# Down-projection of a decoder layer's FFN: 8 block products per pair, or 7 by a Strassen scheme between the next group's up tiles

## The chip, the core and the metric

The kernel runs on one core of one Trainium2 chip. The metric is the device time of one execution in microseconds; lower is better. Five engines work side by side, each through its own instructions in order: TensorE (PE, with its weight loads as PEld), VectorE (DVE), ScalarE (ACT), GpSimd (POOL) and SyncE (SP). SyncE does no arithmetic here, it issues DMAs; the 16 DMA engines of the core move the bytes.

## The reference: one layer with an FFN

One decoder layer over 256 tokens of 2048 channels: a mixing part (convolution, pooling, cross-attention), its output projection, and an FFN with 5632 hidden channels. All is float32. What the change touches is the FFN's last step:

```python
        h = rmsnorm(x, g_ffn[l])
        u = causal_dwconv(h @ w_up[l], ffn_conv_w[l]) + ffn_conv_b[l]
        gate, val = jnp.split(u, 2, axis=-1)
        x = x + (jax.nn.silu(gate) * val) @ w_down[l]
    return rmsnorm(x, g_final)
```

## The kernel before, and how its work is staged

Float32 products are made on TensorE from operands in two float32r parts, hi and lo, with hi x hi + hi x lo + lo x hi, three matmuls for one. Activations stay in SBUF with both parts side by side; weights are streamed. A weight tile of 1 MB (128 x 2048 floats) is loaded by SyncE into one of three `raw` buffers (`load`, L108), then `split_piece` (L121) has ScalarE copy it to `hi` (L129) and VectorE subtract to get `lo` (L130). `hi` and `lo` have three buffers each. `next_tile` (L149) hands tiles out in the order of a list, `stream`, and issues loads three tiles ahead and splits two tiles ahead of use.

The FFN runs over 22 units of 256 hidden channels. `up(u, gi)` makes a unit: four weight tiles, two for the gate and two for the value (`unit_a`, `mm_a`: pairs of a 512-column and a 256-column matmul, L306 and L309), and after each half `up_finish`: copy from PSUM and add (`gather`, L322 to L324), convolution over tokens (L747, L751), silu (L755). The product of gate and value is split and put into the group's tile `u` (L776 to L778). GpSimd sets the two margin columns of each half's rows (L743) in six rotating buffers.

Units form groups of 8, 7, 5 and 2 (`UNITS`, L157). A group's down-projection, `down` (L782), comes after the first unit of the next group, that of the third group after all units. For each half of the 2048 output columns it runs `mm_b` (L326) over tiles of two chunks of 128 hidden channels: 24 matmuls of 512 columns for a tile (L338, L341, L344), with four accumulators in PSUM (two token blocks by two column blocks of 512). At the end of the half `add_in` (L702) adds them to the residual `xt` (L706). The last group of two units goes through `down_last` (L793), with the final norm and the output stores. In between, the scheduler places instructions on each engine by priority; the first and last parts keep the order of the program.

```python
    UNITS = [8, 7, n_units - 17, 2]  # sizes of FFN groups in units of 256 channels
...
    def next_tile():
        i = state["use"]
        state["use"] += 1
        advance(i + 1 + LOAD_AHEAD, i + 1 + SPLIT_AHEAD)
        return split.pop(i)
```

Of the kernel before, what the change touches and what calls it, by code (L numbers as in the profile page):

```python
# [24 lines left out]
def kernel(  # L25
# [45 lines left out]
    # Per-channel vectors, as columns of 128 channels, by transposing rows of 128.  # L71
# [20 lines left out]
    rows = lambda v: v.rearrange("(r c) -> r c", c=P)  # noqa: E731  # L92
# [10 lines left out]
    stream = []  # (source, nk, ncol, pieces)  # L103
# [52 lines left out]
    n_units = NF // 2  # L156
    UNITS = [8, 7, n_units - 17, 2]  # sizes of FFN groups in units of 256 channels  # L157
# [20 lines left out]
    # The pool's weights: per pair of groups the three chunks' rows, in the columns of  # L178
    # the output chunks that they reach; wp_at[k] is the first of them.
# [17 lines left out]
    # Chunks of the mix in the order in which they come about.  # L197
# [10 lines left out]
    # A group's down-projection comes after the next group's first unit; that of the  # L208
    # last but one after all units.
    sched = []  # L210
    done = 0
    for gi, (a, n) in enumerate(group_of):
        upto = n_units if gi + 2 >= len(group_of) else a + n + 1
        for u in range(done, upto):
            sched.append(("up", u, [g for g, (b, m) in enumerate(group_of) if b <= u][-1]))
        done = upto
        sched.append(("down", gi, None))
    for what, a, b in sched:
        if what == "up" and a == 0:
            for h in (0, 1):  # L220
                plan_a(w_up, 0, (h,))
                plan_a(w_up, D_UP, (h,))
        elif what == "up":
            plan_a(w_up, a * 256)
            plan_a(w_up, D_UP + a * 256)
        else:
            a0, n = group_of[a]
            for n2 in range(2):
                plan_b(w_down, a0 * 2, n * 2, n2 * 1024, 1024, 2)

# [89 lines left out]
    def gather(ps, row, o, engine=nc.vector):  # L320
        """(main + corrections) * row -> o [P, S] in SBUF."""
        nc.scalar.activation(o, ps[:, S:], AF.Copy)  # L322
        nc.vector.tensor_tensor(o, ps[:, :S], o, op=ALU.add)
        engine.tensor_tensor(o, o, row, op=ALU.mult)  # L324
# [44 lines left out]
    # The order of the first instructions is that in which the data arrive.  # L369
# [66 lines left out]
    def split_into(o, src, n=S):  # L436
        """float32 [P, n] -> o, its two parts one after the other."""
# [50 lines left out]
    # 1 / (number of tokens averaged) for the first tokens  # L488
# [73 lines left out]
    # The sums run on GpSimd while the next unit's products do; the rest comes after.  # L562
    pending = []

    def pool_sums(ps, i):
# [3 lines left out]
        spans = []  # (first row, last row, group) of this chunk  # L569
# [17 lines left out]
    def pool_means():  # L587
        for i, v, spans, sums in pending:
# [11 lines left out]
            # The convolution's chunks of the mix are free until it comes.  # L600
# [122 lines left out]
    row_2 = None  # L723
    u_tiles = {}

    def up_matmul(u):
        if u:
            return [unit_a(h2T, f"g{u}"), unit_a(h2T, f"v{u}")]
        ps = [[bank(f"pu0_{w}_{mi}") for mi in range(2)] for w in range(2)]
        for h in range(2):  # L730
            for w in range(2):
                mm_a(ps[w], next_tile(), h2T, h * 8, 8, h == 0, h == 1)
                if h == 0 and w == 0:
                    transpose_in(xt, h2T, "g_ffn", range(8, 16), "x2")
        return ps

    def up_finish(ps, u, w):
        """main + corrections, norm, convolution and bias of one half of a unit."""
# [20 lines left out]
    def up(u, gi):  # L759
        nonlocal row_2  # L760
        if gi not in u_tiles:
            u_tiles[gi] = apool.tile([P, 16, 2 * S], F32R, tag="act", name=f"u_{gi}")
        ut = u_tiles[gi]
        base = group_of[gi][0]
        if u == 0:
            ps_g, ps_v = up_matmul(0)
            row_2 = row_of(rstd_sum(ssq4, "x2"), "x2")
            gates = up_finish(ps_g, u, 0)
        else:
            ps_g = unit_a(h2T, f"g{u}")  # L770
            gates = up_finish(ps_g, u, 0)
            ps_v = unit_a(h2T, f"v{u}")
        vals = up_finish(ps_v, u, 1)
        for mi in range(2):
            c = (u - base) * 2 + mi
            nc.vector.tensor_tensor(gates[mi], gates[mi], vals[mi], op=ALU.mult)  # L776
            nc.scalar.activation(ut[:, c, :S], gates[mi], AF.Copy)
            nc.vector.tensor_tensor(  # L778
                ut[:, c, S:], gates[mi], ut[:, c, :S].bitcast(F32), op=ALU.subtract
            )  # L780

    def down(gi):  # L782
        ut = u_tiles[gi]
        nk = group_of[gi][1] * 2
        for n2 in range(2):
            ps = [[bank(f"pd_{gi}_{n2}_{tb}_{n}") for n in range(2)] for tb in range(TB)]
            for i in range(nk // 2):
                mm_b(ps, next_tile(), ut, (2 * i, 2 * i + 1), range(TB), i == 0, i == nk // 2 - 1)
            add_in(ps, n2 * 2, range(TB), f"d{gi}")

    # The last group goes by token blocks and column pieces, each followed by its share
    # of the final norm, so that little is left after the last product.
    def down_last(gi):  # L793
        ut = u_tiles[gi]
# [3 lines left out]
        nc.scalar.activation(gfin, gfin, AF.Copy, scale=-0.5)  # goes with -2 / sqrt  # L798
# [28 lines left out]
        def partial(tb):  # L827
            """The mean square + eps, but for the last piece."""
# [4 lines left out]
        def rstd_last(tb):  # L833
            """-2 / sqrt(mean square + eps), with a Newton step."""
# [20 lines left out]
        with tc.manual_schedule(engines=IN_ORDER):  # L855
# [32 lines left out]
    for what, a, b in sched:  # L888
        if what == "up":
            up(a, b)  # L890
        elif a < len(group_of) - 1:
            down(a)
        else:
            down_last(a)
# [31 lines left out]
```

## Time and profile before

| | before |
|---|---|
| time, median of 3 runs | 1064.57 us (1064.54 to 1064.72) |
| profiled execution: span | 1064.7 us |
| instructions | 14249 |
| moved by DMA | 202.01 MB, 190 GB/s in the mean |
| VectorE, most waited for | lo on ACT's hi: 270.6 us in 168 waits |

The profile comes from one execution. Busy time is given for each engine; the span is cut into 40 slices whose digits are busy tenths; PEclk is the clock granted to TensorE in tenths of full speed. A group row reads: line, engine, operation, what is written and read, shape, count | busy us, mean ns of one | idle time of the engine just before, and what ended it. The chain that ended last follows the work back from the last instruction to whatever released it. No accumulating DMA and no DMA issued by GpSimd is in this profile.

### The profile page before, as it was taken

The page shows a single profiled execution, that of the slowest core. Times are in us where ns is not written, and L with a number is a line of the kernel's source. Part 1 is how long each engine was busy: PE and PEld are TensorE (multiplying, and loading weights), DVE is VectorE, ACT ScalarE, POOL GpSimd, SP SyncE. Part 2 cuts the span into 40 slices and gives each one's busy share as a digit, 9 for nine tenths or more (in the row PEclk, how much of TensorE's full clock was granted, in tenths as well). Part 3 has the DMA queues.
Part 4 walks back from the last instruction along what each step waited for, and adds up shares of the span by engine and source line. Part 5 has one row for each costly group of instructions (what it writes and reads, how often), then busy time and mean ns, then how long its engine had stood idle before and what let it go on. Part 6 is the DMA issues. An engine that isn't in the chain of part 4 may idle for free.

```text
span 1064.7 us, 14249 instructions
## 1 busy us (share of the span) xinstructions
PE 1054.7 (99%) x5632; PEld 907.2 (85%) x5632; DVE 703.6 (66%) x920; ACT 529.0 (50%) x683; POOL 43.1 (4%) x163
## 2 busy tenths in 40 slices
PE   9999999999999999999999999999999999999996
PEld 8888898888888888888888888888888888888885
DVE  5677786764556777777744467777754477777655
ACT  5965454443446655555533344554533345555343
POOL 0023500000000000000000000000000000000000
PEclk9999999999999999999999999999999999999998
DMA  9765465455555556555555555655555555654552
GB/s 316 243 224 172 143 206 189 161 195 183 186 185 174 184 196 198 188 181 185 198 198 198 196 171 187 198 185 175 195 198 197 191 174 190 198 177 178 198 198 80
DMA packets 147342, 202.01 MB, mean 190 GB/s; under 512 B 3619, under 2 KB 125771, under 8 KB 147147
## 3 DMA queue, kind: packets, MB, share of 16 engines
q1 hardware_dynamic: 147242, 201.09, 55.8%
q8 instruction: 44, 0.72, 0.3%
q14 instruction: 24, 0.19, 0.0%
q10 hardware_dynamic: 32, 0.01, 0.0%
HBM read 198.99 MB, written 2.10 MB: 189 GB/s over the span
## 4 chain that ended last, share of the span: by engine, by line
PE 98%; DVE 1%; ACT 0%; issue 0%; DVEq 0%
PE pa_v L306 15%; PE pa_g L306 15%; PE pa_g L309 7%; PE pa_v L309 7%; PE pd L338 7%; PE pd L344 7%; PE pd L341 7%; PE po L338 3%; PE po L341 3%; PE po L344 3%; PE pa_cc L306 2%; PE pa_cx L306 2%; PE pa_cb L306 2%; PE pa_pv L306 2%; PE pk L395 2%; PE pa_q L306 1%
## 5 line engine op out<-in xcount | busy, mean ns | idle before, releaser
L130 DVE TENSOR_TENSOR lo<-raw,hi 128x2048 fp32r<-128x2048 f32 (+2 forms) x196 | 425.5, 2172 | 271.6 <-ACT hi L129 270.6
L129 ACT ACTIVATE hi<-raw 128x2048 fp32r<-128x2048 f32 (+2 forms) x196 | 355.9, 1818 | 255.8 <-PE pd L344 98.4
L306 PE MATMUL pa_v<-h2T,hi 128*128 128x512 f32 x672 | 236.7, 396 | 0.0
L306 PE MATMUL pa_g<-h2T,hi 128*128 128x512 f32 x672 | 236.7, 396 | 0.0
L309 PE MATMUL pa_g<-h2T,lo 128*128 128x256 f32 x672 | 188.5, 281 | 0.0
L309 PE MATMUL pa_v<-h2T,lo 128*128 128x256 f32 x672 | 188.5, 281 | 0.0
L306 PEld LDWEIGHTS pa_v<-h2T,hi 128*128 128x128 f32 x672 | 126.0, 188 | 30.0
L306 PEld LDWEIGHTS pa_g<-h2T,hi 128*128 128x128 f32 x672 | 126.0, 188 | 30.0
L309 PEld LDWEIGHTS pa_g<-h2T,lo 128*128 128x128 f32 x672 | 127.0, 189 | 0.1
L309 PEld LDWEIGHTS pa_v<-h2T,lo 128*128 128x128 f32 x672 | 127.0, 189 | 0.0
L338 PE MATMUL pd<-hi,u 128*128 128x512 f32 x320 | 98.6, 389 | 0.0
L341 PE MATMUL pd<-lo,u 128*128 128x512 f32 x320 | 98.5, 389 | 0.0
L344 PE MATMUL pd<-hi,u 128*128 128x512 f32 x320 | 98.5, 389 | 0.0
L751 DVE SCALAR_TENSOR_TENSOR t<-h,cols,t 128x256 f32<-128x256 f32 x176 | 79.1, 480 | 2.2 <-ACT t L747 1.4
L755 ACT ACTIVATE t<-t 128x256 f32<-128x256 f32 x44 | 18.3, 418 | 107.0 <-DVE t L751 107.0
L341 PEld LDWEIGHTS pd<-lo,u 128*128 128x128 f32 x320 | 60.1, 188 | 12.6
L344 PEld LDWEIGHTS pd<-hi,u 128*128 128x128 f32 x320 | 60.1, 188 | 12.4
L338 PEld LDWEIGHTS pd<-hi,u 128*128 128x128 f32 x320 | 59.9, 188 | 12.4
L747 ACT ACTIVATE t<-h,cols 128x256 f32<-128x256 f32 x88 | 49.8, 593 | 0.0
L322 ACT ACTIVATE h<-pa_g 128x256 f32<-128x256 f32 x42 | 16.0, 380 | 61.3 <-PE pa_g L309 61.3
L338 PE MATMUL po<-hi,mixT 128*128 128x512 f32 x128 | 39.6, 391 | 0.0
L341 PE MATMUL po<-lo,mixT 128*128 128x512 f32 x128 | 39.5, 389 | 0.0
(207 smaller groups left out, 1280.9 us busy)
## 6 DMA issues: line engine op xcount, KB each, us to landing
raw<-in_w_up_dram SPq DMA_DIRECT2D x88, 1024.0 KB, 5.0
raw<-in_w_down_dram SPq DMA_DIRECT2D x44, 1024.0 KB, 4.9
raw<-in_w_in_dram SPq DMA_DIRECT2D x28, 1024.0 KB, 4.9
raw<-in_w_out_dram SPq DMA_DIRECT2D x16, 1024.0 KB, 4.9
raw<-in_w_kv_dram SPq DMA_DIRECT2D x4, 1024.0 KB, 5.2
raw<-in_w_kv_dram SPq DMA_DIRECT2D x6, 512.0 KB, 8.3
memt<-in_mem_dram SPq DMA_DIRECT2D x8, 256.0 KB, 7.7
xt<-in_x_dram SPq DMA_DIRECT2D x4, 512.0 KB, 6.7
```

The lines of the kernel that those rows point to most:

```text
L129: nc.scalar.activation(hi[:, s, :], raw[:, s, :], AF.Copy)
L130: nc.vector.tensor_tensor(lo[:, s, :], raw[:, s, :], hi[:, s, :].bitcast(F32), op=ALU.subtract)
L306: nc.tensor.matmul(ps[mi], hi[:, kk, c], actT[:, k, :], start=first and kk == 0, stop=False)
L309: nc.tensor.matmul(ps[mi][:, S:], lo[:, kk, c], actT[:, k, :S], start=False, stop=last and kk == nk - 1,)
L322: nc.scalar.activation(o, ps[:, S:], AF.Copy)
L338: nc.tensor.matmul(ps[tb][n], ah, hi[:, kk, c], start=f, stop=False)
L341: nc.tensor.matmul(ps[tb][n], ah, lo[:, kk, c], start=False, stop=False)
L344: nc.tensor.matmul(ps[tb][n], al, hi[:, kk, c], start=False, stop=l)
L395: nc.tensor.matmul(psk[mi], wt[0][:, j, c], mT[:, k, :], start=k == 0, stop=False)
L747: nc.scalar.activation(t, hp[:, 2:], AF.Identity, bias=cvec("ffn_conv_b", m), scale=cw[2])
L751: nc.vector.scalar_tensor_tensor(t, hp[:, s : s + S], cw[s], t, op0=ALU.mult, op1=ALU.add)
L755: nc.scalar.activation(t, t, AF.Silu)
```

## The change

The FFN's groups become five of 4 units and a last one of 2. For each of the five groups the down-projection is done in two halves of 1024 columns (`Blocks`, p = 0 and 1). In each, the activations are taken as 2 x 2 blocks (two token blocks of 128; even and odd chunks of hidden channels, four chunks each), and so are the weights (even and odd chunks; two column blocks of 512). Instead of 8 block products 7 are made, each of 4 chunks x 3 matmuls of 512 columns. The left operands are sums and differences of activation blocks, made by `turn` on VectorE and ScalarE once per group into the tile `sums`; the right ones are sums of weight blocks, made in place in three 1 MB buffers of the tile `ffn` by DMAs from SBUF to SBUF that add to their destination, issued by GpSimd:

| product | left | right | buffer steps after its split |
|---|---|---|---|
| 0 | a11 | b11 | b11 += b12; b12 += b22 |
| 1 | a21 - a22 | b11 + b12 | b11 += b22 |
| 2 | a21 - a22 - a11 | b11 + b12 + b22 | |
| 3 | a11 - a21 | b12 + b22 | load b21 over b12; b11 += b21 |
| 4 | a12 + a21 - a22 - a11 | b22 | load the next pair's b11 |
| 5 | a12 | b21 | load the next pair's b22 |
| 6 | a22 | b11 + b12 + b22 + b21 | load the next pair's b12 |

Each product's PSUM bank is added to or subtracted from a block of `xt` right away; some products go on in the bank of an earlier one. A group's 14 products stand between the next group's 16 up tiles: none after the first three, one after each of the next twelve, two after the last. In the last group, which has eight up tiles, it is one after each of six, two after the seventh and six after the eighth. The comments are left out too.

```diff
     def load(i, between=None):
         src, nk, ncol, pieces = stream[i]
+        if nk is None:
+            return
...
-    UNITS = [8, 7, n_units - 17, 2]  # sizes of FFN groups in units of 256 channels
+    UNITS = [4] * ((n_units - 2) // 4) + [2]
...
+        def buf(self, name):
+            at = {"b11": 0, "b22": 1, "b12": 2, "b21": 2}[name]
+            return rawd[(self.seq + at) % 3]
...
+        def add(self, to, what):
+            nc.gpsimd.dma_start(self.buf(to), self.buf(what), accum_op=ALU.add)
+
+        def split(self, i, idx):
+            raw = self.buf(("b11", "b11", "b11", "b12", "b22", "b21", "b11")[idx])
+            hi, lo = split[i] = [
+                wpool.tile([P, 4, 512], F32R, tag=t, name=f"{t}_{i}") for t in ("hi", "lo")
+            ]
+            nc.scalar.activation(hi, raw, AF.Copy)
+            nc.vector.tensor_tensor(lo, raw, hi.bitcast(F32), op=ALU.subtract)
+            if idx == 0:
+                self.add("b11", "b12")
+                self.add("b12", "b22")
+            elif idx == 1:
+                self.add("b11", "b22")
+            elif idx == 3:
+                self.load("b21")
+                self.add("b11", "b21")
+            elif self.next is not None and idx >= 4:
+                self.next.load({4: "b11", 5: "b22", 6: "b12"}[idx])
...
+        if not prods:
+            after = [0] * n_t
+        elif n == 4:
+            after = [0, 0, 0] + [1] * 12 + [2]
+        else:
+            after = [1, 1, 1, 1, 1, 1, 2, 6]
...
+        for at, src in parts:
+            nc.scalar.activation(sums[:, at, 0], src, AF.Copy)
+        tt(t[:, 0], a21, a22, op=ALU.subtract)
+        tt(t[:, 2], a11, a21, op=ALU.subtract)
+        tt(t[:, 1], t[:, 0], a11, op=ALU.subtract)
+        for at, src in parts[:1]:
+            tt(sums[:, at, 1], src, sums[:, at, 0].bitcast(F32), op=ALU.subtract)
+        tt(t[:, 3], t[:, 1], a12, op=ALU.add)
+        nc.scalar.activation(sums[:, 1:5, 0], t, AF.Copy)
+        for at, src in parts[1:]:
+            tt(sums[:, at, 1], src, sums[:, at, 0].bitcast(F32), op=ALU.subtract)
+        tt(sums[:, 1:5, 1], t, sums[:, 1:5, 0].bitcast(F32), op=ALU.subtract)
...
+    def prod(bl, i):
+        hi, lo = next_tile()
...
+        for j in range(4):
+            ah, al = sums[:, i, 0, j, :], sums[:, i, 1, j, :]
+            for n, (a, b) in enumerate(((ah, hi), (ah, lo), (al, hi))):
+                nc.tensor.matmul(
+                    ps, a, b[:, j, :], start=first and j == 0 and n == 0,
+                    stop=j == 3 and n == 2, skip_group_check=True,
+                )
+        c0 = bl.p * 1024 + right * 512
+        o = xt[:, tb, c0 : c0 + 512]
+        nc.vector.tensor_tensor(o, o, ps, op=op)
```

How the instructions then stand is decided by the scheduler. On ScalarE, in the middle of the FFN, this is the stretch of one unit before: `hi` is a weight split, `h` the copy from PSUM, `t` the convolution or silu. In brackets are the semaphores waited for; DMAHW are the loads.

```order
L322 ACTIVATE h_0_0_4157<-pa_g_0_4079 128x256 [waits PE_49,Pool_49]
L129 ACTIVATE hi_4181<-raw_4119 128x2048 [waits DMAHW3_49,PE_49,Activation_49]
L747 ACTIVATE t_0_0_4162<-h_0_0_4157,cols 128x256 [waits DVE_49]
L322 ACTIVATE h_0_1_4167<-pa_g_1_4080 128x256 [waits PE_49,Pool_49]
L755 ACTIVATE t_0_0_4162<-t_0_0_4162 128x256 [waits DVE_49]
L129 ACTIVATE hi_4219<-raw_4179 128x2048 [waits DMAHW4_49,PE_49,Activation_49]
```

The same engine after the change, at the first three products of a group's first pair. L131 splits an up tile, L247 a product's weight block out of the tile `ffn`; DMASW are the adding DMAs that GpSimd issued.

```order
L247 ACTIVATE hi_4837<-ffn 128x2048 [waits DMAHW1_49,Activation_49]
L131 ACTIVATE hi_4875<-raw_4835 128x2048 [waits DVE_49,DMAHW6_49,PE_49,Activation_49]
L808 ACTIVATE t_0_0_4818<-h_0_0_4813,cols 128x256 [waits DVE_49]
L808 ACTIVATE t_0_1_4828<-h_0_1_4823,cols 128x256 [waits DVE_49]
L816 ACTIVATE t_0_0_4818<-t_0_0_4818 128x256 [waits DVE_49]
L816 ACTIVATE t_0_1_4828<-t_0_1_4828 128x256 [waits DVE_49]
L387 ACTIVATE h_1_0_4911<-pu_1_0_4833 128x256 [waits PE_49,Pool_49]
L387 ACTIVATE h_1_1_4920<-pu_1_1_4834 128x256 [waits PE_49,Pool_49]
L808 ACTIVATE t_1_0_4916<-h_1_0_4911,cols 128x256 [waits DVE_49]
L808 ACTIVATE t_1_1_4925<-h_1_1_4920,cols 128x256 [waits DVE_49]
L247 ACTIVATE hi_4933<-ffn 128x2048 [waits DMASW0_49,Activation_49]
L131 ACTIVATE hi_4954<-raw_4931 128x2048 [waits DMAHW7_49,PE_49,Activation_49]
```

A product's split now stands ahead of each up tile's split, and that of product 1 (hi_4933) waits for an adding DMA, with the next up tile's split behind it.

On GpSimd there were only the margins of the up rows (L743) in this part. Now the adds (L240) stand among them (L804), here those of a first pair's products 0 and 1:

```order
L240 DMA ffn<-ffn 128x2048 [waits DMAHW5_49,DMAHW3_49,DMAHW7_49,DMAHW0_49,DVE_49]
L804 MEMSET h_1_0_4124 128x2 [waits DVE_49,Activation_49,Pool_49]
L804 MEMSET h_1_1_4133 128x2 [waits DVE_49,Activation_49,Pool_49]
L240 DMA ffn<-ffn 128x2048 [waits DMAHW1_49,DMASW0_49]
L804 MEMSET h_0_0_4259 128x2 [waits DVE_49,Activation_49,Pool_49]
L804 MEMSET h_0_1_4269 128x2 [waits DVE_49,Activation_49,Pool_49]
L240 DMA ffn<-ffn 128x2048 [waits DVE_49]
```

The second add (b12 += b22) waits until the first (b11 += b12) has landed, the third (b11 += b22) for VectorE's split of product 1.

At the end of the FFN, ScalarE's row of splits for the last pair, products 1 to 6, and the first tile of the last group's down-projection (L131); L387 and L808 belong to the last up tile, L503 splits the last units' result:

```order
L247 ACTIVATE hi_8370<-ffn 128x2048 [waits DMASW4_49,PE_49,Activation_49]
L387 ACTIVATE h_1_0_8425<-pu_1_0_8311 128x256 [waits PE_49,Pool_49]
L387 ACTIVATE h_1_1_8434<-pu_1_1_8312 128x256 [waits PE_49,Pool_49]
L808 ACTIVATE t_1_0_8430<-h_1_0_8425,cols 128x256 [waits DVE_49]
L808 ACTIVATE t_1_1_8439<-h_1_1_8434,cols 128x256 [waits DVE_49]
L503 ACTIVATE h2T<-t_0_0_8277 128x256 [waits DVE_49]
L247 ACTIVATE hi_8389<-ffn 128x2048 [waits DMASW6_49,Activation_49]
L503 ACTIVATE h2T<-t_0_1_8287 128x256 [waits DVE_49]
L247 ACTIVATE hi_8453<-ffn 128x2048 [waits DMASW5_49,Activation_49]
L247 ACTIVATE hi_8473<-ffn 128x2048 [waits DMAHW5_49,PE_49,Activation_49]
L247 ACTIVATE hi_8490<-ffn 128x2048 [waits DMAHW1_49,DVE_49,PE_49]
L247 ACTIVATE hi_8509<-ffn 128x2048 [waits DMASW7_49,DVE_49,PE_49]
```

Products 1, 2, 3 and 6 wait for adds (DMASW), and no up tile's split stands between them; the last group's tiles come behind.

More of the change, by code (lines that the diff above doesn't have):

```diff
@@ L156 @@
     n_units = NF // 2
[L157 removed]
+    UNITS = [4] * ((n_units - 2) // 4) + [2]
+    assert sum(UNITS) == n_units
     D_UP = DFF
@@ L210 @@
+    blocks = []
+    for gi in range(len(group_of) - 1):
+        for p in range(2):
+            blocks.append(Blocks(len(blocks), gi, p))
+            if len(blocks) > 1:
+                blocks[-2].next = blocks[-1]
     sched = []
-    done = 0
+    prods = []
     for gi, (a, n) in enumerate(group_of):
[L213 to L217, printed above, removed]
@@ L218 @@
-    for what, a, b in sched:
[L219 to L229, printed above, removed]
+        n_t = 4 * n
+        if not prods:
[4 more added lines that the diff above has]
+            after = [1, 1, 1, 1, 1, 1, 2, 6]
@@ new lines @@
+        assert sum(after) == len(prods)
+        for t in range(n_t):
+            sched.append(("up", a + t // 4, t % 4))
+            for _ in range(after[t]):
+                sched.append(prods.pop(0))
+        if gi < len(group_of) - 1:
+            sched.append(("turn", gi, None))
+            prods = [("prod", b, i) for b in blocks[2 * gi : 2 * gi + 2] for i in range(N_PROD)]
+    for what, a, b in sched:
+        if what == "up":
+            w, h = (b % 2, b // 2) if a == 0 else (b // 2, b % 2)
+            plan_a(w_up, w * D_UP + a * 256, (h,))
+        elif what == "prod":
+            stream.append((a, None, b, 1))
@@ L232, in turn_pair @@
+    a0, n = group_of[-1]
+    for n2 in range(2):
+        plan_b(w_down, a0 * 2, n * 2, n2 * 1024, 1024, 2)
     def turn_pair(xt, k, nm):
@@ L723 @@
     row_2 = None
[L724 to L735, printed above, removed]
+    sums = apool.tile([P, N_PROD + 1, 2, 4, P], F32R, tag="act", name="sums")
+    ffn = apool.tile([P, 4, 2048], F32, tag="act", name="ffn")
+    u_raw = ffn[:, 0, :].rearrange("p (c t) -> p c t", t=S)
+    rawd = [ffn[:, 1 + i, :].rearrange("p (j c) -> p j c", c=512) for i in range(3)]
+    for name in ("b11", "b22", "b12"):
+        blocks[0].load(name)
+    u_last = h2T[:, : 2 * UNITS[-1], :]
     def up_finish(ps, u, w):
@@ L757, in up_finish, with up @@
         return outs
-    def up(u, gi):
+    up_ps, up_gates = {}, {}
+    def up(u, b):
         nonlocal row_2
[L761 to L766, printed above, removed]
-            row_2 = row_of(rstd_sum(ssq4, "x2"), "x2")
[L768 to L773, printed above, removed]
-        for mi in range(2):
[L775 to L789, printed above, removed]
+        w, h = (b % 2, b // 2) if u == 0 else (b // 2, b % 2)
+        if h == 0:
+            up_ps[w] = [bank(f"pu{u}_{w}_{mi}") for mi in range(2)]
@@ new lines, in up @@
+        mm_a(up_ps[w], next_tile(), h2T, h * 8, 8, h == 0, h == 1)
+        if u == 0 and b == 0:
+            transpose_in(xt, h2T, "g_ffn", range(8, 16), "x2")
+        if h == 0:
+            return
+        if u == 0 and w == 0:
+            row_2 = row_of(rstd_sum(ssq4, "x2"), "x2")
+        done = up_finish(up_ps.pop(w), u, w)
+        if w == 0:
+            up_gates[u] = done
+            return
+        gates = up_gates.pop(u)
+        last = u >= group_of[-1][0]
+        for mi in range(2):
+            c = (u % 4) * 2 + mi
+            if not last:
+                nc.vector.tensor_tensor(u_raw[:, c, :], gates[mi], done[mi], op=ALU.mult)
+                continue
+            nc.vector.tensor_tensor(gates[mi], gates[mi], done[mi], op=ALU.mult)
+            pending_u.append((c, gates[mi]))
@@ new lines, in up, with turn @@
+        if u == n_units - 1:
+            for c, t in pending_u:
+                split_into(u_last[:, c, :], t)
+    pending_u = []
+    def turn(gi):
+        v = u_raw.rearrange("p (j s) (b t) -> p s b j t", s=2, b=TB)
+        a11, a12, a21, a22 = v[:, 0, 0], v[:, 1, 0], v[:, 0, 1], v[:, 1, 1]
+        t = wpool.tile([P, 4, 4, P], F32, tag="raw", name=f"turn_{gi}")
+        tt = nc.vector.tensor_tensor
+        parts = [(0, a11), (5, a12), (6, a22)]
+        for at, src in parts:
[10 more added lines that the diff above has]
+        tt(sums[:, 1:5, 1], t, sums[:, 1:5, 0].bitcast(F32), op=ALU.subtract)
@@ new lines @@
+    chains = {}
+    def prod(bl, i):
+        hi, lo = next_tile()
+        chain, first, tb, right, op = (
+            ("a", True, 0, 0, ALU.add),
+            ("b", True, 1, 1, ALU.add),
+            ("a", False, 0, 1, ALU.subtract),
+            ("a", False, 1, 1, ALU.subtract),
+            ("b", False, 0, 1, ALU.add),
+            ("c", True, 0, 0, ALU.add),
+            ("a", False, 1, 0, ALU.add),
+        )[i]
+        if first:
+            chains[chain] = bank(f"pp_{bl.seq}_{chain}")
+        ps = chains[chain]
+        for j in range(4):
[8 more added lines that the diff above has]
+        nc.vector.tensor_tensor(o, o, ps, op=op)
@@ L888 @@
     for what, a, b in sched:
[L889 to L894, printed above, removed]
+        {"up": up, "turn": lambda g, _: turn(g), "prod": prod}[what](a, b)
+    down_last(len(group_of) - 1)
 _INS = [
```

17 lines of the change are left out of this document (16 added, 1 removed).

## The prediction

> **What bounds the kernel now.** I read the busy shares first, then the slices, then the chain of waits that ended last.
>
> ```profile
> span 1064.7 us, 14249 instructions
> PE 1054.7 (99%) x5632; PEld 907.2 (85%) x5632; DVE 703.6 (66%) x920; ACT 529.0 (50%) x683; POOL 43.1 (4%) x163
> PE   9999999999999999999999999999999999999996
> PEclk9999999999999999999999999999999999999998
> PE 98%; DVE 1%; ACT 0%; issue 0%; DVEq 0%
> ```
>
> TensorE is busy in every slice but the last, at its full granted clock, and 98% of the chain is its own work: the time is a sum of matmuls. The span (1064.7) lies within 0.2 us of the median of the runs (1064.57), so nothing lies around it and I add to and take from 1064.7. The pace of the two kinds of stage comes from the windows view (per engine: busy us and, in brackets, instructions; then the clock and the busy share of the 16 DMA engines), one stretch of up tiles and one of down-projection:
>
> ```profile
> core 0: us, PE busy (x) PEld busy (x) DVE busy (x) ACT busy (x) POOL busy (x), PEclk, DMA share, GB/s
> 360.00:520.00 160.00, 160.00 (x925) 141.06 (x924) 119.61 (x172) 85.94 (x114) 2.90 (x29) 1.00 0.57 191
> 522.00:610.00 88.00, 88.00 (x391) 72.91 (x390) 45.30 (x37) 33.77 (x24) 0.30 (x3) 1.00 0.56 193
> ```
>
> Down-projection: 88/391 = 0.225 us for a matmul of 512 columns. Up: 160/925 = 0.173 us in the mean of 512 and 256 columns, so an up tile of 32 matmuls (half a unit's gate or value) takes 5.54 us.
>
> **The change: what TensorE saves.** The first 40 of 44 chunks go from 8 block products to 7.
>
> ```profile
> L338 PE MATMUL pd<-hi,u 128*128 128x512 f32 x320 | 98.6, 389 | 0.0
> L341 PE MATMUL pd<-lo,u 128*128 128x512 f32 x320 | 98.5, 389 | 0.0
> L344 PE MATMUL pd<-hi,u 128*128 128x512 f32 x320 | 98.5, 389 | 0.0
> ```
>
> That is 960 matmuls; the new 5 groups x 2 column halves x 7 products x 12 matmuls are 840. 120 x 0.225 = **27.0 us saved**; up tiles, head and last group keep their matmuls. A product of 12 takes 2.70 us, and the usual beat, an up tile and a product, 8.24 us.
>
> **What the other engines get.** The products need 70 splits of 128x2048 where 40 tiles were split, 70 additions into xt for 24, and five turns.
>
> ```profile
> L130 DVE TENSOR_TENSOR lo<-raw,hi 128x2048 fp32r<-128x2048 f32 x175 | 401.4, 2294 | 264.8 <-ACT hi L129 264.5
> L751 DVE SCALAR_TENSOR_TENSOR t<-h,cols,t 128x256 f32<-128x256 f32 x176 | 79.1, 480 | 2.2 <-ACT t L747 1.4
> L324 DVE TENSOR_TENSOR h<-h,row_x 128x256 f32<-128x256 f32 x88 | 35.4, 421 | 0.8
> L323 DVE TENSOR_TENSOR h<-pa_g,h 128x256 f32<-128x256 f32 x42 | 17.7, 422 | 18.7 <-ACT h L322 18.5
> L776 DVE TENSOR_TENSOR t<-t,t 128x256 f32<-128x256 f32 x44 | 16.8, 420 | 0.0
> L706 DVE TENSOR_TENSOR xt<-pd,xt 128x512 f32<-128x512 f32 x24 | 14.9, 683 | 0.0
> ```
>
> For one full group (16 up tiles, 14 products; TensorE 16 x 5.54 + 14 x 2.70 = 126.4 us) VectorE has 16 x 2.29 for the up splits, 14 x (2.29 + 0.68) for products, (79.1 + 35.4 + 2 x 17.7 + 16.8)/22 = 7.6 per unit x 4 for norm, convolution and gating, and 7 x 0.68 + 2.29 for the turn: 116 us, 92%. ScalarE has less. So both still fit beneath TensorE, with VectorE near its limit; I price this at nothing, and its cover is the 10 us a group that VectorE has left. The turn has three up tiles (16.6 us) before the first product needs it; it costs nothing either. The three first block loads join SyncE's queue at the end of the output projection, where they wait only for attention to be long done: nothing.
>
> **The accumulating DMAs.** This is what I think decides. Within a pair the second product's weight block is b11 + b12, the third's that plus b22, both made in place. The chain is: split product 0 (ScalarE, then VectorE), GpSimd issues the add, it lands, split product 1, the next add, split product 2. No trace row shows an accumulating DMA, or one from SBUF to SBUF. The nearest are the weight loads, also 1 MB, from issue to landing:
>
> ```profile
> raw<-in_w_up_dram SPq DMA_DIRECT2D x88, 1024.0 KB, 5.0
> DMA to landing us min/median/max: 4.0/4.9/8.5
> q1 hardware_dynamic: 147242, 201.09, 55.8%
> ```
>
> From the last row, 1 MB (1.049 MB in its units) costs 0.558 x 1064.7 x 1.049/201.09 = 3.1 us of all 16 DMA engines, which leaves 1.9 us of the landing as latency. If an add is no dearer than a load, T, its time from issue to landing, is 4.0 to 5.0. If it must read both operands, T = 1.9 + 2 x 3.1 = 8.1. If a load shares the engines for its whole length, 11.2. I take **8.1**: an add has two inputs, and nothing else in a row prices the second one. Both ends stay for the range.
>
> [...]
>
> How long may an add take unnoticed? Splitting takes, in the timeline (start, length):
>
> ```profile
> 945.58 1.91 ACT L129 ACTIVATE hi<-raw 128x2048 fp32r<-128x2048 f32 x1
> 947.52 2.29 DVE L130 TENSOR_TENSOR lo<-raw,hi 128x2048 fp32r<-128x2048 f32 x1 [0.92 <-ACT hi L129]
> ```
>
> 949.81 - 945.58 = 4.2 us, with the hand-over from the DMA 4.3. With three hi/lo buffers a split may begin one beat before its product: when the tile three back is done, at 0, ScalarE first copies from PSUM, the split ends near 5.0, and the product starts at 8.2: 3.2 us early. On the other beat, behind the gate work on VectorE, about 2.3 early. I take a lead of 2.5 us. So product 1 is late by T + 4.3 - 8.24 - 2.5 = T - 6.4; after that no lead is left and product 2 is late by T - 3.9. At 8.1: 1.7 + 4.2 = 5.9 us a pair. GpSimd's other add (b12 += b22) waits for the first to land and is needed two beats later: hidden. Behind each waiting hi split on ScalarE stand the next up tile's hi split and then the copies of finished up tiles; they catch up during the 2.70 us of the product. Behind the waiting DMA on GpSimd stand two margin memsets, used a gate half later: free. The b21 chain (load 5.0, add 8.1, split 4.3: 17.4) has three beats, 24.7: hidden. Nine of the ten pairs are like this: 9 x 5.9 = **53 us**.
>
> **The last pair** has no up tiles left between its products: six follow the last one. Time 0 is the end of the seventh tile of the last group; two products and an up tile end at 10.9. b12 can load only when product 6 of the pair before has been split (-2.3, landing 2.7). The first add lands at 10.8, product 1 starts at 15.1 (4.2 late) and ends at 17.8. The second lands at 23.2, product 2 starts at 27.5 (9.7 late), ends at 30.2, with product 3's split right behind. b21 loads 30 to 35, product 5 starts at 39.2 (3.5 late), the last add lands at 43.1 and product 6 starts at 47.4 (5.5 late). The last group's tiles stand behind it on every engine. Sum **22.9 us**.
>
> **Sum:** 1064.7 - 27.0 + 53 + 22.9 = **1114 us**.
>
> **The rivals.**
>
> *The adds land like loads (faster).* T = 5.0: product 1 is 1.4 early, product 2 is still in time (5.0 - 3.9 - 1.4 < 0). Only the last pair stalls, 1.1 + 6.6 + 3.4 + 2.3 = 13.4. 1064.7 - 27.0 + 13.4 = 1051; at T = 4.0 some 3 us less. For it: loads do land in 4.9 with the engines over half busy. Against: two inputs, and a GpSimd queue that the trace has never used. The sign turns where 9 x (2T - 10.3) and the tail together eat 27: T near 5.8. That the products would not stand between the up tiles at all is ruled out by the rows of ScalarE's order shown with the change.
>
> *The DMA engines fill up.* A group now moves 24 loads x 3.1 = 74 us and, at double cost, 8 adds x 6.2 = 50: 124 of 126 us. The order on GpSimd puts b12 += b22 right where the second critical add follows. With T = 9.7 for the first and 11.2 for the second, a pair loses 3.3 + 7.3 = 10.6, the tail 29: 1064.7 - 27 + 95 + 29 = 1162.
>
> *The clock drops in the gaps.* Before, TensorE never pauses until its last matmul, and then:
>
> ```profile
> 1055.00:1060.00 5.00, 0.98 (x9) 0.78 (x7) 4.59 (x13) 1.28 (x6) 0.00 (x0) 0.85 0.52 197
> 1060.00:1064.00 4.00, 0.00 (x0) 0.00 (x0) 1.04 (x2) 0.00 (x0) 0.00 (x0) 0.50 0.61 234
> 6.78 2.04 PE L395 MATMUL pk<-mT,hi 128*128 128x512 f32 x4 [0.26 <-DVE mT L249]
> 13.71 1.08 PE L395 MATMUL pk<-mT,hi 128*128 128x512 f32 x4
> ```
>
> 0.85 over five microseconds means full until about 1058.5, some 2.5 us after the last matmul, then half. At the start four matmuls take 2.04 us, later 1.08; the slow ones last some 3.5 us, a loss of about 1.7. My forecast has 13 gaps of 3.5 us and more: 13 x 1.7 = 22, so 1136. [...]
>
> *VectorE becomes the bound.* Up tiles before leave it (160 - 119.6)/7.2 = 5.6 us idle a unit, mostly behind ScalarE's hi. If that idle stays, a unit takes 116/4 + 5.6 = 34.6 against TensorE's 31.6: 3 us x 16 units = 48. With quick adds 1064.7 - 27 + 48 + 13 = 1099. Against: much of that idle is slack waiting for a buffer, which goes when work is there.
>
> **Chances.** Forecast 0.35, full DMA engines 0.20, clock 0.11, VectorE 0.05, adds like loads 0.25. Measuring can tell about 0.2% (2.1 us) from no change; only T near 5.8 ends there, 0.04. So faster 0.25, same 0.04, slower 0.71. The range takes in quick adds, down to 1046, and full engines with some clock loss, up to 1172; the slower cases alone span 1080 (T = 6.5) to 1172.
>
> **What would show it.** ScalarE's product hi (L247) waiting for an add for several us twice a pair, and TensorE idle before products 1 and 2 alone: the chain. Adds landing in about 8 us: the price; in 5 or less: wrong, and no idle between up tiles. 840 product matmuls at 0.225: the saving. A gap of some 23 us in all before the last group: the tail. Granted clock under 1.00 inside the FFN: the clock rival. Landing times of w_up loads well above 5.0: full engines. VectorE above 95% busy: its rival. A loss outside the FFN would be none of my steps.

## The result and the profile after

| | before | after |
|---|---|---|
| time, median of 4 runs each | 1064.64 us | 1148.28 us (1147.51 to 1148.52) |
| ratio, 95% interval | | 1.0782 [1.0766, 1.0797] |
| span of the profiled execution | 1064.7 us | 1146.0 us |
| TensorE busy / idle | 1054.7 / 10.0 us | 1063.8 / 82.2 us |

The kernel is 7.8% slower. The page of the changed kernel, the lines that answer to those of before (busy, slices, granted clock, the chain that ended last by engine):

```profile
span 1146.0 us, 14222 instructions
PE 1063.8 (93%) x5512; PEld 900.3 (79%) x5512; DVE 814.1 (71%) x996; ACT 592.5 (52%) x693; POOL 77.4 (7%) x203
PE   9999999999999997998989989899899897979676
PEclk9999999999999999998999989989899998989879
PE 66%; DMA 17%; DVE 9%; ACT 5%; issue 2%; POOL 0%; DVEq 0%; ACTq 0%; POOLq 0%
```

TensorE has 120 matmuls fewer and is yet busy 9.1 us longer, and it stands idle for 72 us more. Both begin where the products begin. The windows view shows the last stretch of up tiles alone, a stretch with products, and the end:

```profile
325.00:420.00 95.00, 95.00 (x554) 83.92 (x553) 70.61 (x102) 50.88 (x69) 1.95 (x18) 1.00 0.54 176
420.00:560.00 140.00, 127.61 (x644) 106.73 (x644) 103.35 (x116) 74.78 (x72) 8.50 (x23) 0.96 0.82 225
1080.00:1146.00 66.00, 43.61 (x183) 34.02 (x181) 38.65 (x50) 27.24 (x36) 0.86 (x1) 0.84 0.35 108
```

The granted clock (third number from the right) goes with the idle: 1.00, 0.96, 0.84; the last row takes in the 8.6 us after the last matmul. What TensorE waits for stands in the chain, followed in order of time through the first pair (start, length):

```profile
428.19 2.21 DVE lo L248
430.40 0.31 issue
430.71 8.29 DMA ffn<-ffn
...
439.08 1.92 ACT hi L247
...
441.03 2.30 DVE lo L248
443.33 0.29 issue
443.62 9.14 DMA ffn<-ffn
...
452.87 1.92 ACT hi L247
454.79 0.02 issue
454.81 1.78 DVE lo L248
```

Split, add, split, add, split: from the end of product 0's split (430.40) to the end of product 2's (456.59) are 26.2 us, where TensorE's own work between the two products is two beats, 16.5. The adds over the whole run (their queue's share of 16 engines; the median and the range from issue to landing), the up tiles' loads beside them, and the waits:

```profile
q0 software_dynamic: 5760, 41.95, 19.3%
DMA to landing us min/median/max: 6.9/8.4/14.0
raw<-in_w_up_dram SPq DMA_DIRECT2D x88, 1024.0 KB, 6.4
ACT hi L247 <- DMA ffn<-ffn: 123.0, 20, 10.3
PE pp_a L897 <- ACT hi L247: 40.2, 11, 6.8
PE pp_a L897 <- DVE lo L248: 10.1, 6, 1.8
```

ScalarE waits for an add 20 times, twice in each of ten pairs, and the largest of TensorE's waits stand at bank pp_a, whose second product is product 2. By the timeline product 1 is late only in the first pair behind a turn, by 1.4 to 1.8 us in four of the five groups, and in the last pair; product 2 is late in every pair, by 4.1 to 5.9 us in the first nine.

For what follows I cut the time at two fixed points: the turns. The first and the last `turn` begin at 417.3 and 999.1, with four groups between them, so a group takes 145.5 us; from the last turn to the end are 146.9 us.

```profile
L866 DVE TENSOR_TENSOR turn<-ffn x5: 682/683/687, 417.3 to 999.1; 128x512 f32<-128x512 f32 x5
```

### The profile page after: what moved, and what is told of

Its sections match the earlier page's. It is cut to its first block, busy times and chain, and to the rows that moved or that the text cites. A ratio compares the mean times of both kernels' runs of the same rounds, so it can differ in the third digit from the quotient of the medians.

```text
span 1146.0 us, 14222 instructions
## 1 busy us (share of the span) xinstructions
PE 1063.8 (93%) x5512; PEld 900.3 (79%) x5512; DVE 814.1 (71%) x996; ACT 592.5 (52%) x693; POOL 77.4 (7%) x203
## 4 chain that ended last, share of the span: by engine, by line
PE 66%; DMA 17%; DVE 9%; ACT 5%; issue 2%; POOL 0%; DVEq 0%; ACTq 0%; POOLq 0%
PE pu L371 17%; DMA ffn<-ffn 16%; PE pu L374 9%; PE pp_a L897 6%; DVE lo L248 6%; ACT hi L247 4%; PE po L406 3%; PE po L403 3%; PE po L409 3%; PE pp_b L897 2%; PE pa_cx L371 2%; PE pa_cc L371 2%; PE pa_cb L371 2%; PE pa_pv L371 2%; PE pp_c L897 1%
## 5 line engine op out<-in xcount | busy, mean ns | idle before, releaser
L371 PE MATMUL pu<-h2T,hi 128*128 128x512 f32 x1408 | 500.6, 399 | 6.3 <-ACT hi L131 6.3
L132 DVE TENSOR_TENSOR lo<-raw,hi 128x2048 fp32r<-128x2048 f32 (+3 forms) x156 | 333.2, 2138 | 104.4 <-ACT hi L131 103.5
L374 PE MATMUL pu<-h2T,lo 128*128 128x256 f32 x1408 | 393.8, 281 | 3.3 <-DVE lo L132 3.3
L131 ACT ACTIVATE hi<-raw 128x2048 fp32r<-128x2048 f32 (+3 forms) x156 | 278.8, 1791 | 130.2 <-PE po L409 39.3
L371 PEld LDWEIGHTS pu<-h2T,hi 128*128 128x128 f32 x1408 | 265.4, 189 | 70.1 <-ACT hi L131 8.1
L374 PEld LDWEIGHTS pu<-h2T,lo 128*128 128x128 f32 x1408 | 266.7, 190 | 8.2 <-DVE lo L132 5.4
L248 DVE TENSOR_TENSOR lo<-ffn,hi 128x2048 fp32r<-128x2048 f32 x70 | 160.3, 2290 | 113.1 <-ACT hi L247 113.0
L247 ACT ACTIVATE hi<-ffn 128x2048 fp32r<-128x2048 f32 x70 | 133.8, 1912 | 160.8 <-DMA ffn<-ffn 123.0
L897 PE MATMUL pp_a<-hi,sums 128*128 128x512 f32 x320 | 120.8, 442 | 40.2 <-ACT hi L247 40.2
L897 PE MATMUL pp_a<-lo,sums 128*128 128x512 f32 x160 | 71.8, 449 | 10.1 <-DVE lo L248 10.1
L387 ACT ACTIVATE h<-pu 128x256 f32<-128x256 f32 x88 | 32.0, 377 | 78.7 <-PE pu L374 78.7
L808 ACT ACTIVATE t<-h,cols 128x256 f32<-128x256 f32 x88 | 50.0, 592 | 26.1 <-DVE h L389 26.1
L240 POOL DMA_DIRECT2D ffn<-ffn x40 | 34.5, 864 | 360.7 <-DVE lo L248 141.8
L804 POOL MEMSET h<- 128x2 f32 x88 | 11.2, 145 | 472.0 <-DVE t L812 368.5
```

Of the source, the lines that this page charges most:

```text
L131: nc.scalar.activation(hi[:, s, :], raw[:, s, :], AF.Copy)
L132: nc.vector.tensor_tensor(lo[:, s, :], raw[:, s, :], hi[:, s, :].bitcast(F32), op=ALU.subtract)
L247: nc.scalar.activation(hi, raw, AF.Copy)
L248: nc.vector.tensor_tensor(lo, raw, hi.bitcast(F32), op=ALU.subtract)
L371: nc.tensor.matmul(ps[mi], hi[:, kk, c], actT[:, k, :], start=first and kk == 0, stop=False)
L374: nc.tensor.matmul(ps[mi][:, S:], lo[:, kk, c], actT[:, k, :S], start=False, stop=last and kk == nk - 1,)
```

## The experiments

My theory was the one of the prediction, with the clock added: products 1 and 2 wait for their adds, and each wait also costs clock. The rivals were the load of the adds on the DMA engines, and VectorE as the bound. Every run, by the same cut:

| run | time | a group | last turn to end | adds land (median) |
|---|---|---|---|---|
| the change | 1148.28 | 145.5 | 146.9 | 8.4 |
| e1 no adds | 1048.69 | 128.4 | 116.1 | |
| e2 adds where nobody waits early | 1076.12 | 131.5 | 131.2 | 8.9 |
| e3 half of each add | 1080.69 | 132.2 | 131.0 | 5.3 |
| e4 copies | 1067.16 | 129.2 | 129.0 | 5.7 |
| e5 filler matmuls | 1134.79 | 142.1 | 147.4 | 8.7 |
| e6 adds on GpSimd | 1166.23 | 152.5 | 137.3 | (5.3, busy) |
| e7 reordered | 1079.53 | 130.6 | 138.0 | 8.4 |
| e8 and spread | 1072.94 | 130.1 | 133.6 | 8.2 |
| e9 and one add on VectorE | 1065.97 | 129.7 | 127.7 | 8.1 |
| e10 only in the last group | 1066.75 | 129.7 | 126.6 | 8.2 |
| e11 last group plain | 1054.46 | 129.4 | | 8.1 |

A time for which the text gives no interval is that of a single run, and the cuts come from one profile of each kernel. The ten runs of e10 lie 6.6 us apart, so a difference of that size between single runs, as between e7 and e8, is hardly clear of the noise.

**e1: no adds.**

```diff
         def add(self, to, what):
-            nc.gpsimd.dma_start(self.buf(to), self.buf(what), accum_op=ALU.add)
+            return
```

> Left out: all 40 accumulating transfers, so products 1, 2, 3 and 6 use single weight blocks in place of sums. Chain theory (products 1 and 2 wait for the add): the waits go, and with them the gaps that cost the clock; the forecast's 1064.7 - 27 and a few us at the last pair, 1038 to 1050 us, TensorE idle under 25 us, granted clock 0.99 or more. VectorE-bound rival: the FFN still holds at VectorE's 116 us per group with its queueing, 1080 to 1099. If some cost of the change lies outside the adds (turn, loads by halves), it is what remains above 1040.

1048.69 us, the busy row and the turns:

```profile
PE 1031.0 (98%) x5512; PEld 882.3 (84%) x5512; DVE 814.0 (78%) x996; ACT 594.1 (57%) x693; POOL 43.1 (4%) x163
L866 DVE TENSOR_TENSOR turn<-ffn x5: 681/685/687, 417.2 to 930.8; 128x512 f32<-128x512 f32 x5
560.00:705.00 145.00, 144.88 (x766) 123.40 (x765) 127.63 (x145) 86.92 (x85) 2.01 (x20) 1.00 0.60 190
```

Everything that was lost hangs on the 40 adds: 99.1 us of span. With the same 5512 matmuls TensorE is idle 1046.9 - 1031.0 = 15.9 us in place of 82.2, and busy 32.8 us less. So 66.3 us of the loss are waits and 32.8 are the same work done slower. In the third row TensorE works 144.88 of 145 us with VectorE at 127.63 (88%): VectorE is not the bound, and its rival falls.

**e2: the same transfers, no early wait.**

```diff
             if idx == 0:
-                self.add("b11", "b12")
+                self.add("b12", "b11")
                 self.add("b12", "b22")
-            elif idx == 1:
+            elif idx == 2:
                 self.add("b11", "b22")
```

> The same 40 transfers of 1 MB, same queue, but none that products 1 and 2 wait for: b12+=b11 and b12+=b22 behind split 0, b11+=b22 behind split 2, b11+=b21 behind split 3; left out are the sums in products 1 and 2. Chain theory: like without adds, 1040 to 1055, as the first consumer (product 3) has three beats of 8.24 us for two adds of 8.4. Rival that the adds take the DMA engines from the weight loads (5.5 us of all 16 engines each, 44 us per group): the time stays between 1110 and 1148, with TensorE waiting for w_up splits.

1076.12: neither number. The steady part answers clearly, by its turns and the loads of the up tiles (the last two rows are of the timeline, near the end: start, length, and in brackets the idle time before):

```profile
L866 DVE TENSOR_TENSOR turn<-ffn x5: 681/684/685, 417.3 to 943.1; 128x512 f32<-128x512 f32 x5
raw<-in_w_up_dram SPq DMA_DIRECT2D x88, 1024.0 KB, 7.2
...
1018.59 1.91 ACT L247 ACTIVATE hi<-ffn 128x2048 fp32r<-128x2048 f32 x1 [12.72 <-DMA ffn<-ffn]
...
1025.36 0.77 PE L897 MATMUL pp_b<-hi,sums 128*128 128x512 f32 x1 [14.17 <-ACT h2T L503]
```

With all 40 transfers on the engines, landing in 8.9 and holding up the weights to 7.2, a group takes 131.5: 3.1 us over the kernel without adds, against 17.1 for the change. So of 17.1 us a group, at most 3.1 are load on the DMA engines and 14.0 go with the place of the waits. Of the 27.4 us that the run takes more than e1, four groups make 12.2, so it would stand near 1061 and above its forecast even without its last group; that adds the other 15.1. There two adds now follow one another ahead of product 3, with no up tiles left to cover them: ScalarE's split of it waits 12.7 us, the next product's split stands behind it, and TensorE is still for 14.2 us (the row names the instruction of ScalarE that ended last before it; VectorE's additions into `xt` of products 1 and 2, which free their banks, stand behind the late split as well).

**e3 and e4: what an add is made of.** e3 adds two of the four chunks, e4 copies in place of adding.

```diff
-            nc.gpsimd.dma_start(self.buf(to), self.buf(what), accum_op=ALU.add)
+            nc.gpsimd.dma_start(self.buf(to), self.buf(what))
```

> The adds become plain copies of the same 1 MB between the same buffers on the same queue, with the same waits; the sums are left out. If the second input of the accumulation is what makes an add long, a copy lands in 5 to 6.4 us like a load, product 1 is not late and product 2 by at most 2.5 us per pair: 1040 to 1075. If a transfer from SBUF to SBUF on this queue is long by itself, it lands in about 8 us and the time stays at 1130 to 1148.

> Each add covers two of the four chunks (0.5 MB in place of 1 MB); the sums are left out in the other half. An add should land about 5.5 us after issue (estimate: 2.5 fixed and half of the rest of 8.4). Chain theory: product 1 no longer late (5.5 - 6.4 < 0), product 2 late by 5.5 - 3.9 = 1.6 us per pair, some 16 us over ten pairs and some 8 us of clock: 1050 to 1070. DMA-engine rival: half of the cost of the adds stays, about 1094. A fixed time per add as the main cost would leave it above 1120.

The queue's share and the landing, first e4, then e3:

```profile
q0 software_dynamic: 5760, 41.95, 10.0%
DMA to landing us min/median/max: 4.2/5.7/10.1
...
q0 software_dynamic: 5760, 20.97, 10.4%
DMA to landing us min/median/max: 4.5/5.3/10.0
```

A copy takes 0.100 x 1065.0/40 = 2.7 us of all 16 engines and lands in 5.7; the add of the same megabyte takes 0.193 x 1146.0/40 = 5.5 and lands in 8.4. The second input costs 2.8 us of engine time and 2.7 us of landing. e4 came out as expected (1067.16). e3 did not (1080.69, where 1050 to 1070 was expected): its adds land sooner than the copies (5.3 against 5.7; of the 2.5 us estimated as fixed, half and whole adds leave 2 x 5.3 - 8.4 = 2.2), and yet it takes 13.5 us more. In the pair behind a turn the second link of its chain leaves later. The timeline shows product 1's split there, in e3 and then in e4:

```profile
701.92 1.92 ACT L249 ACTIVATE hi<-ffn 128x2048 fp32r<-128x2048 f32 x1 [2.27 <-DMA ffn<-ffn]
704.42 1.77 DVE L814 SCALAR_TENSOR_TENSOR t<-h,cols,t 128x256 f32<-128x256 f32 x4 [1.78 <-ACT t L810]
706.78 2.29 DVE L250 TENSOR_TENSOR lo<-ffn,hi 128x2048 fp32r<-128x2048 f32 x1
...
697.59 1.93 ACT L247 ACTIVATE hi<-ffn 128x2048 fp32r<-128x2048 f32 x1 [0.20 <-DMA ffn<-ffn]
700.11 2.28 DVE L248 TENSOR_TENSOR lo<-ffn,hi 128x2048 fp32r<-128x2048 f32 x1
```

In e3 ScalarE's hi ends at 703.84, but VectorE takes up four convolution instructions first and reaches its part 2.9 us later; in e4 it does so 0.6 us behind. So part of the wait is VectorE's order of work and not the transfer. Why the order comes out so in the one and not in the other I did not follow further.

**e5: filler for the clock.**

```diff
+        if i == 2:
+            chains["c"] = bank(f"pp_{bl.seq}_c")
+            for _ in range(16):
+                nc.tensor.matmul(
+                    chains["c"], h2T[:, 15, :P], h2T[:, 15, :], start=True, stop=True
+                )
```

> The changed kernel with 16 more 128x512 matmuls (3.6 us at 0.225) ahead of product 2 of every pair, into a bank that product 5 clears later; they need no weights of the pair, so they run while TensorE waits for the second add. Clock theory (the time lost beyond the gaps, some 36 us, is the clock that falls behind each gap): the granted clock in the FFN rises from 0.96 to about 1.00 and the time falls by 15 to 35 us, 1113 to 1133, though no add becomes faster. If the 36 us have another cause (weight loads, VectorE), the filler changes nothing: 1145 to 1151. If the gaps are shorter than 3.6 us on average, the filler itself shows: above 1151.

1134.79, ratio to before 1.0659 [1.0613, 1.0705]: 13.5 us faster than the change with 160 matmuls more, and adds that land no sooner (8.7).

```profile
PE 1086.7 (96%) x5672; PEld 920.7 (81%) x5672; DVE 812.6 (72%) x996; ACT 593.1 (52%) x693; POOL 77.4 (7%) x203
560.00:705.00 145.00, 140.81 (x737) 119.19 (x736) 113.69 (x131) 77.85 (x77) 8.42 (x24) 1.00 0.84 237
```

Without the filler's 160 x 0.225 = 36.0 us TensorE is busy 1050.7, 13.1 less than in the change for the same work; idle is 46.4, less by the 35.8 that the filler fills. In this window the clock is 1.00, where the change had 0.96. So the clock theory holds for these 13 us. The expected gain of 15 to 35 was missed narrowly: it is 3.4 us a group, the last group gains nothing, and 1050.7 - 1031.0 = 19.7 us of slower work remain that this run does not undo.

The rest can be read from the clock of the change itself. The windows view, cut where the granted clock changes, gives 0.50 in 13 stretches of 3.41, 6.83 or 10.24 us; the last row is the sum over the 13. The first two rows are the time before one of them and the stretch itself, the third is the least idle time that brought a fall, the fourth the most that brought none:

```profile
599.70:603.12 3.42, 0.49 (x1) 0.19 (x1) 1.60 (x1) 3.42 (x2) 0.00 (x0) 1.00 0.51 178
603.10:606.51 3.41, 3.17 (x8) 2.50 (x9) 3.41 (x4) 2.53 (x4) 0.00 (x0) 0.50 0.00 0
1002.48:1005.90 3.42, 1.48 (x9) 1.34 (x10) 2.28 (x2) 2.34 (x2) 0.86 (x1) 1.00 0.27 50
1101.50:1104.91 3.41, 1.75 (x8) 1.45 (x9) 2.21 (x2) 0.00 (x0) 0.00 (x0) 1.00 0.99 202
sum 75.08, PE 57.47 PEld 43.48 DVE 66.49 ACT 45.02 POOL 1.31; mean PE 4.42 PEld 3.34 DVE 5.11 ACT 3.46 POOL 0.10
```

TensorE worked 57.47 us at half clock, a loss of 28.7. The same reading gives 30.28 us in e5 (15.1 lost; granted clock 0.983 over its span) and 3.42 in e1 (1.7; 0.996). So 27.0 of the 32.8 us of slower work are clock, and e5 took back 13.6 of them, about what its busy time says (13.1). Each of the nine waits for product 2 before the last pair brought such a stretch. Cut into pieces of 3.41 us in step with these stretches, this run shows the clock fall after each piece at full clock in which TensorE stood idle 1.9 us or more, and after none with 1.7 or less.

**e6: the adds on GpSimd itself.**

```diff
-            nc.gpsimd.dma_start(self.buf(to), self.buf(what), accum_op=ALU.add)
+            to, what = self.buf(to), self.buf(what)
+            nc.gpsimd.tensor_tensor(to, to, what, op=ALU.add)
```

> The 40 adds of blocks as GpSimd instructions (128x2048) in place of transfers, same order, same waits. From this kernel's rows (128x256 adds on GpSimd 0.62 to 0.85 us) an add should take 5.0 to 6.8 us and leave the DMA engines alone. Chain theory: product 1 hardly late, product 2 by 1 to 3 us per pair: 1055 to 1085, between the plain copies (1067) and the half adds (1081). If GpSimd slows VectorE, or the margins' memsets queue behind the adds, it stays above 1090.

1166.23, the second case. The adds take what was expected of them, and ScalarE's waits for them fall from 123.0 us to 34.6; the groups of VectorE tell the rest:

```profile
L241 POOL TENSOR_TENSOR ffn<-ffn 128x2048 f32<-128x2048 f32 x40 | 212.0, 5301 | 233.9 <-DVE lo L249 130.4 <-DMA ffn<-in_w_down_dram 88.9 <-DVE xt L904 14.1
L813 DVE SCALAR_TENSOR_TENSOR t<-h,cols,t 128x256 f32<-128x256 f32 x176 | 154.4, 891 | 4.7 <-ACT t L809 4.1
L390 DVE TENSOR_TENSOR h<-h,row_x 128x256 f32<-128x256 f32 x88 | 51.7, 597 | 1.2
L389 DVE TENSOR_TENSOR h<-pu,h 128x256 f32<-128x256 f32 x88 | 36.0, 419 | 25.1 <-ACT h L388 25.1
PE pu L375 <- DVE lo L132: 62.0, 18, 6.3
```

The convolution's instructions go from 480 to 891 ns in the mean and the product with the row from 421 to 597, while the sum with a PSUM operand stays at 419 (420 in the change). VectorE is busy 135 of 145 us in the steady windows, and TensorE waits for its splits of up weights (62.0 us). Here TensorE waits for VectorE: the cover that the prediction priced at nothing is gone.

**e7 to e10: the same adds with more time.** e7 makes the products in the order 0, 4, 1, 5, 2, 3, 6. Between two products whose weights stand in the same b11 buffer there is then always another, which needs no sum of it. Product 4 gets a bank of its own, product 1's result is added to both token blocks, and b21 comes as an ordinary streamed tile.

```diff
+    ORDER = (0, 4, 1, 5, 2, 3, 6)
...
-            elif idx == 3:
-                self.load("b21")
+            elif idx == 2:
                 self.add("b11", "b21")
-            elif self.next is not None and idx >= 4:
-                self.next.load({4: "b11", 5: "b22", 6: "b12"}[idx])
+            if self.next is not None and idx in (2, 3, 6):
+                self.next.load({2: "b11", 3: "b22", 6: "b12"}[idx])
...
-            ("b", False, 0, 1, ALU.add),
+            ("d", True, 0, 1, ALU.add),
...
+        for t in (1, 0) if i == 1 else (tb,):
```

> All adds and sums as in the changed kernel, products in the order 0, 4, 1, 5, 2, 3, 6, so that every add on b11 has two beats (16.5 us) in place of one; product 4 gets its own bank (one more addition of 128x512 per pair), b21 comes through the buffers of the up tiles. Chain theory: the waits go in the steady part, what stays is the load on the DMA engines (about 3 us per group, from the moved adds) and the last pair, whose products still stand without up tiles between them: 1068 to 1085. DMA-engine rival: 1110 or more.

> As the reordered kernel, with the last group's 14 products spread 2, 2, 2, 2, 2, 2, 1, 1 over its eight up tiles in place of 1 x6, 2, 6. Chain theory: each add has 10.9 us or more at the end too, so the last group loses its gaps: 8 to 15 us less than the reordered kernel, 1057 to 1072. If the end is bound by something else (the split of the last weights, the token-block order of the last down-projection), no difference.

e7: 1079.53, as expected. A group takes 130.6 us with adds that land in 8.4 as before:

```profile
L876 DVE TENSOR_TENSOR turn<-ffn x5: 684/684/690, 417.3 to 939.8; 128x512 f32<-128x512 f32 x5
ffn<-ffn POOLq DMA_DIRECT2D x30, 1024.0 KB, 8.4
```

e8 changes the last group's list:

```diff
-            after = [1, 1, 1, 1, 1, 1, 2, 6]
+            after = [2, 2, 2, 2, 2, 2, 1, 1]
```

It gains 6.6 (8 to 15 were expected); one add in the last pair still takes 12 us to land, and TensorE waits 5.8 and 1.5 us at its product 1:

```profile
PE pp_b L907 <- ACT hi L255: 5.8, 1, 5.8
PE pp_b L907 <- DVE lo L256: 1.5, 1, 1.5
```

e9 then puts b11 += b22 on VectorE in all pairs, and e10 instead both links of the chain in the last two pairs alone (the edit shown is that of e9):

```diff
             elif idx == 1:
-                self.add("b11", "b22")
+                to, what = self.buf("b11"), self.buf("b22")
+                nc.vector.tensor_tensor(to, to, what, op=ALU.add)
```

> The reordered, spread kernel with b11+=b22 on VectorE (128x2048, 2.29 us like its other such rows) in place of a transfer, in all pairs: ten transfers fewer, 11 us of the DMA engines per group less, 4.6 us of VectorE per group more (about 122 of 130). If what is left over the kernel without adds (1073 against 1049) is load on the DMA engines, it gains 3 to 10 us, 1063 to 1070. If VectorE is then what bounds the group, it is the same or slower: 1072 to 1085, with TensorE waiting for splits of up weights.

> The reordered, spread kernel with b11+=b12 and b11+=b22 on VectorE in the last two pairs alone (4 adds, 9.2 us of VectorE in the last group; 4 transfers fewer). The time from the last turn to the end is 133.6 us there and 116.1 without adds; if the last pair's transfers (one took 12 us to land, and a wait of 5.8 and 1.5 us followed) are that difference, it falls by 6 to 12 us: 1061 to 1067. If VectorE then holds up the last group, no gain or a loss: 1071 to 1080.

1065.97 (1.001 [1.0, 1.0021]) and 1066.75 (1.0017 [1.0003, 1.0031]): as expected, and level with before within 0.2%. A group is 0.4 us shorter in both, although e10 leaves its transfers there as they were, so ten transfers fewer bring nothing that shows; the end gains 5.9 in e9 and 7.0 in e10. What was left by then was mostly the last group, not the load on the DMA engines in the steady part.

**e11: the last group without sums.** The last four-unit group's down-projection goes as eight plain block products, one weight block and both token blocks at a time, on top of e9.

```diff
+    def plain(bl, at):
+        h, s = at
+        hi, lo = next_tile()
+        for tb in range(TB):
+            if s == 0:
+                chains[tb] = bank(f"pq_{bl.p}_{h}_{tb}")
+            for j in range(4):
+                ah, al = sums[:, 2 * tb + s, 0, j, :], sums[:, 2 * tb + s, 1, j, :]
...
-            after = [2, 2, 2, 2, 2, 2, 1, 1]
+            after = [1, 1, 1, 1, 1, 1, 1, 1]
```

> A version meant to beat both: the kernel with one add per pair on VectorE, and the last four-unit group's down-projection as eight plain block products (24 matmuls per weight block, no sums, no adds) in place of fourteen, one block per up tile. TensorE pays 2 x 2.7 = 5.4 us more there; the eight adds, their waits and six weight splits go. Chain theory: the time from the last turn to the end falls from 127.7 to about 121.5 (116.1 without adds, and 5.4), so 1058 to 1062 us, 0.2 to 0.6% under before. If the end is bound by the final weights' loads and splits rather than by the adds, the 5.4 us are added: 1068 to 1072.

```profile
span 1052.7 us, 14211 instructions
PE 1036.3 (98%) x5536; PEld 886.8 (84%) x5536; DVE 814.3 (77%) x996; ACT 581.3 (55%) x687; POOL 64.0 (6%) x187
```

1054.46 us, ratio 0.9901 [0.9884, 0.9917]: 1.0% faster than before, and 3.5 us below the range expected. TensorE is idle for 16.4 us, about as in the kernel without any adds (15.9), at a granted clock of 0.998. This is the version that beats both.

## Why the prediction came out as it did

Slower was right, by the mechanism that it named; the time was 1148.3 where it said 1114, inside the range. In the terms of its sum the rows give 1064.7 - 23.7 (work saved, by e1) + 72.2 (more idle time) + 32.8 (the same work done slower) = 1146.0. It had 27.0, 75.9 and nothing. The first two errors, 3.3 and 3.7 us, cancel by luck, and the third is the miss.

- *27.0 us saved.* 5632 - 5512 = 120 matmuls went. Without adds TensorE is busy 1054.7 - 1031.0 = 23.7 us less than before. Of the missing 3.3 us, 1.7 are e1's one stretch at half clock; what the other 1.6 are is not shown. Right.
- *VectorE and ScalarE priced at nothing.* e1 shows it: TensorE never waits for them in the steady part. e6 shows what the cover was worth.
- *T = 8.1 from two inputs.* 8.4 was measured, and e4 shows the second input by itself (5.7 to 8.4). Right for the reason given, with some luck in the sizes: an input costs 2.7 to 2.8 us of engine time, not 3.1, and what is left of the landing is 2.9 (8.4 - 5.5), not 1.9.
- *5.9 us of waits a pair.* From 420 to 990 TensorE is idle 570 - 523.9 = 46.1 us; a pair takes 72.7 of them, so 46.1 x 72.7/570 = 5.9. The sum was right; its parts were less so. In these nine pairs product 1's waits add up to 6.7 us, 0.7 a pair (forecast 1.7), and product 2 carries 4.9 (4.2). The lead was taken as 2.5 us everywhere; in the first group product 0's split was done 1.7 us ahead in the first pair and 4.0 in the second, where product 1 then was in time. Why the lead differs is not shown.
- *The last group: 5.9 and 22.9, 28.8 us.* Measured against e1, the stretch behind the last turn lost 30.8 us, but some 21 of them are idle; of the other 10, 9.2 are clock. So the waits were forecast 8 us too high: the last pair's alone came to 17.0.
- *The clock left out of the sum.* This is the step that failed. The prediction had the clock as a rival, worked out as 22 on top of the chain, 1136, the nearest of its times, and gave it 0.11 of the chance; its sum has nothing for it. The same matmuls took 32.8 us longer than without the adds, 27.0 of them at half clock (e5 took 13 back); the other 5.8 are open. The prediction's own row had half clock 2.5 us after the last matmul, and the 13 gaps it counted were all longer than that; in the change a single wait of 2.6 us, behind the last turn, was followed by half clock (the third row of the clock above). The 13 gaps came nearly as counted: 12 of the 13 stretches stand at them, one behind the last turn. But each cost 2.2 us in the mean, not 1.7.
- *The rival of full engines.* 124 of 126 us a group were forecast at double cost. The engines were busy 0.82 to 0.83 of the 145.5 us, 120 us: the load was as forecast, but the longer group leaves room for it. The up loads went from 5.0 to 6.4, and e2 and e7 price that load at no more than 2 to 3 us a group. It is there, and small.
- *The rival of quick adds.* e4 is nearly that kernel: at 5.7 it stands 2.3 us above before (1067.16 against 1064.83, one run of each), where the prediction put the turn of the sign near 5.8.

## What to carry to other kernels

A transfer that prepares the very next operand is priced by its distance: count the work between the instruction that issues it and the one that needs it, and reorder the independent products until each has more than its landing time; here that gave back 69 of the 84 us lost, with the adds as slow as before (8.4 us). Price a recurring gap on TensorE at more than its length where the granted clock falls behind it: here 66 us of waits came with 33 us of slower work, 27 of them by the clock, which stood at 0.50 in 13 stretches of 3.41 to 10.24 us; the least idle time that brought it down in the run of the change was 1.9 us within 3.41. Where a scheme saves work only if other work covers its preparation, leave it out at the end of the kernel, where that cover runs out: the plain last group cost 5.4 us of matmuls and gained 11.5.

## What the hardware showed beside that

In e6, with its adds on GpSimd (5.30 us in the mean for 128x2048), some of VectorE's instructions took longer than in the change, by the means of their rows: the convolution 891 ns against 479, the product with the row 597 against 421, the subtraction for lo 2661 against 2290 on an up weight and 2359 against 2290 on a product's block. Others did not: the sum with a PSUM operand 419 against 420, the product of gate and value 419 in both. Nor was each convolution instruction slow: from 400 to 545 us of e6's timeline those listed singly took 0.47 to 0.48 us but for two, of 4.49 and 4.83. GpSimd's issue of an accumulating transfer took 0.86 us, that of a copy 0.53.
